# The end of the first expert stage without GpSimd, and the general expert pass in loops

## The chip, the core and the metric

The kernel runs on one core of a Trainium2 chip. A core has five engines that run side by side, each with its own queue: TensorE (PE in the profile; its weight loads are PEld), VectorE (DVE), ScalarE (ACT), GpSimd (POOL) and SyncE (SP, which here only issues DMAs). They meet through semaphores. TensorE multiplies into PSUM, which GpSimd can't read; SBUF holds everything else. The metric is the device time of one execution in microseconds.

## The reference, cut to what matters

A two-layer network works on 256 latent tokens and 256 context tokens of width 1024. Each layer has a mixer (a convolution, an mLSTM and an RG-LRU side by side) and then a mixture of 16 experts, of which each token uses two. The last layer computes the latent tokens alone. What the change touches is the expert part and the sum around it:

```python
def hier_moe(h, w_rg, b_rg, w_re, b_re, w_gate, w_up, w_down):
    ...
    combine = jnp.sum(jax.nn.one_hot(expert_id, N_EXPERTS) * top_w[..., None], axis=1)
    y = jnp.zeros(hf.shape, jnp.float32)
    for e in range(N_EXPERTS):
        ye = (jax.nn.silu(hf @ w_gate[e]) * (hf @ w_up[e])) @ w_down[e]
        y = y + combine[:, e:e + 1] * ye
...
    h_lat = h_lat + mod_lat[5] * hier_moe(v_lat, *moe_p)
    if not last:
        ...
        h_ctx = h_ctx + mod_ctx[5] * hier_moe(v_ctx, *moe_p)
return rms_norm(h_lat, final_g)
```

Everything is float32. `mod[5]` is a gate, one row of 1024 for the latent tokens and one for the context tokens; `h` on the left is the residual.

## The kernel before

The program is written out in the order mixer 0, experts 0, mixer 1, experts 1. Only TensorE's order is the order of the code (`manual_schedule` for PE); the orders of the other engines are made by a planner at build time, from its own costs, with here and there a constraint by hand: `behind(ins)` puts the instructions of a block behind given instructions on the same engine. A `tc.If` over all engines is a border that the planner moves nothing across.

**Tiles.** Tokens lie in tiles of 128: `NT` is 4 in the first expert stage (two of latent tokens, `m = 0`, and two of context tokens, `m = 1`) and 2 in the second. `hs[m]` holds the residual. `bank()` hands out PSUM banks, six in turn in the first stage and four in the second.

**An expert.** The loop over `x` takes the 16 experts one by one. Each has up to 128 slots: its tokens are gathered by a matmul with a one-hot matrix (`gather`, L1253), multiplied with the gate and up weights (`gu`, L1367), evacuated (`evac`), turned (`act`: transposes L1390, Silu, product L1402) and multiplied with the down weights (`down`, L1416). Groups of slots beyond the first 32 or 64 stand in a `tc.If` on the expert's count, on TensorE alone (L1624, L1631, L1637, L1640, L1663, L1670). `store` copies the result and writes it to DRAM (`Yd`) by DMAs of GpSimd's queue (L1484). Weights come through buffers of several kinds, loaded by SP (`ahead`, L1133, L1139) as earlier contents are released.

**The general pass.** Should an expert have more than 128 tokens, `overflow` computes the rest in full, under `tc.If(n_any > P)` (L1490), over all engines. With these inputs no expert has, so the body is jumped over, in both stages. It stands behind expert `OVER = 3`, after its down matmuls, its stores and the loads of later weights, and `gate_rows` (L265, L266), which makes the gate's rows `gr`, stands just ahead of it.

**The stage's end.** The last expert (`wide`) isn't stored. At its start `fetch` (L1566) begins to gather each token's two rows from `Yd` into `yas[i]`; in the first stage two splits of the next mixer's first weights are prepared too: a split makes a rounded high part (ScalarE's copy, L192) and the rest (a subtraction, L192), its first half of rows on VectorE and its second on GpSimd (`whalf`). `take` weighs and adds the two rows (ScalarE L1582, VectorE L1585), multiplies by the gate's row (VectorE L1587) and adds the residual on GpSimd (L1588). The last expert's own result stays in PSUM (`Z`, by `down_w`, L1452); `spread_y` multiplies it by the gate's row into `yt` (VectorE, L1460), and `to_tokens` turns slots into tokens with a one-hot matmul (L1474) and adds this to what `take` left (VectorE, L1476). In the first stage this is done for `m = 0`, then for `m = 1`; the sums of squares (ScalarE, L1702), the normalization (L277, L278, L279, L284) and the transposes of the next layer (L292) follow, with pieces of the modulation (`pump`: matmuls L234 on weights from `w_mod`, loaded by SP's L188) between them. At the end of the kernel the same steps stand written out (L1730, L1731), and the final norm follows.

Where a helper writes an instruction, the profile shows the helper's line.

Of the kernel before, what the change touches and what calls it, by code (L numbers as in the profile page):

```python
# [40 lines left out]
def hybrid_kernel(ctx, tc, x, c, cx, c_ctx, w_mod, b_mod, norm1_g, norm2_g, w_in, conv_w, conv_b, conv_ln_g,  # L41
# [15 lines left out]
    Yd = dram.tile([NE - NPE, P, D], F32, name="Yd", tag="Yd")  # L57
    cnt = [0]
# [1038 lines left out]
    def moe(l, hs, fill):  # L1097
# [4 lines left out]
        with tc.tile_pool(name=f"mo{l}", bufs=1, reuse_waits="tile") as mo, \  # L1102
# [361 lines left out]
            def totals():  # L1464

                return [yas[i][:, 0] if yas and i < taken[0] else hs[i // 2][:, i % 2] for i in range(NT)]
# [20 lines left out]
            def overflow():  # L1487

                n_any = nc.values_load(cnti[0:1, NE:NE + 1], min_val=0, max_val=NTOK)
                with tc.If(n_any > P):  # L1490
                    cw = mt("cw", [P, NT, NE + 1])
                    cw2 = mt("cw2", [P, NT, NE])
                    fh = tmp.tile([P, 2, 512], F32, yp, f"fh{l}")
                    V.memset(cw, 0.0)
                    V.scalar_tensor_tensor(cw[:, :, 0:NE], pm1, float(P) + 0.5, Wt, op0=OP.is_gt, op1=OP.mult)
                    with tc.For_i(0, NE, 1) as ei:
                        def lw(w, k, c0, res=None):
                            wn[0] += 1
                            t = tmp.tile([P, 512], F32, "Y", f"w{wn[0]}")
                            if res is None:  # L1500
                                src = w[l][bass.ds(ei, 1), k * P:k * P + P, c0:c0 + 512].rearrange("o p f -> p (o f)")
                            else:
                                src = w[l][bass.ds(ei, 1)].rearrange("o (h p k) f -> h k p (o f)", h=2, k=4)[k // 4, k % 4]
                            nc.gpsimd.dma_start(t, src)
                            return t

                        for m in range(NT // 2):
                            for w in (w_gate, w_up):
                                pw = [bank(), bank()]
                                for k in range(KC):  # L1510
                                    wk = lw(w, k, 0, 4)
                                    vn = tmp.tile([P, 2, P], F32, "sg", f"vn{m}{k}", 2)
                                    sl = slice(k * P, k * P + P)
                                    ts = slice(2 * m, 2 * m + 2)
                                    V.tensor_tensor(vn, vh[:, ts, sl].bitcast(F32), vl[:, ts, sl].bitcast(F32),
                                                    op=OP.add)
                                    ps = bank([P, 2, P])
                                    for i in range(2):
                                        T.transpose(ps[:, i, :], vn[:, i, :], ident)
                                    vk = tmp.tile([P, 2, P], F32, "hT", f"vk{m}{k}", 3)  # L1520
                                    V.tensor_copy(vk, ps)
                                    for i in range(2):
                                        T.matmul(pw[i], vk[:, i, :], wk, start=(k == 0), stop=(k == KC - 1))
                                for i in range(2):
                                    if w is w_gate:
                                        S.activation(fh[:, i], pw[i], AF.Silu)
                                    else:
                                        V.tensor_tensor(fh[:, i], fh[:, i], pw[i], op=OP.mult)
                            hts = []
                            for i in range(2):  # L1530
                                V.tensor_scalar(fh[:, i], fh[:, i], cw[:, 2 * m + i, 0:1], None, op0=OP.mult)
                                pt = bank()
                                for f in range(4):
                                    T.transpose(pt[:, f * P:f * P + P], fh[:, i, f * P:f * P + P], ident)
                                ht = tmp.tile([P, 512], F32, "t2", f"ft{m}{i}")
                                V.tensor_copy(ht, pt)
                                hts.append(ht)
                            for hf in range(2):
                                py = [bank(), bank()]
                                for k in range(4):  # L1540
                                    wk = lw(w_down, k, 512 * hf)
                                    for i in range(2):
                                        T.matmul(py[i], hts[i][:, k * P:k * P + P], wk, start=(k == 0), stop=(k == 3))
                                sl = slice(512 * hf, 512 * hf + 512)
                                for i in range(2):
                                    hh = hs[m][:, i, sl]
                                    yt = tmp.tile([P, 512], F32, "t2", f"fy{m}{hf}{i}")
                                    V.tensor_tensor(yt, py[i], gr[m][:, sl], op=OP.mult)
                                    V.tensor_tensor(hh, hh, yt, op=OP.add)
                        V.tensor_copy(cw2, cw[:, :, 1:NE + 1])  # L1550
                        V.tensor_copy(cw[:, :, 0:NE], cw2)
# [26 lines left out]
            def take(ts, ws2):  # L1578
                taken[0] += len(ts)
                for i in ts:  # L1580
                    h, y = hs[i // 2][:, i % 2, :], yas[i]
# [14 lines left out]
            for x in range(NE):  # L1596
# [79 lines left out]
                if x == OVER:  # L1676
                    gr = gate_rows(l, 5, mo, "gr", range(NT // 2), NT // 2)
                    overflow()

            if not last:  # L1680
# [4 lines left out]
                g23 = gate((2, 3))  # L1685
                for m in range(2):
# [33 lines left out]
            if last:  # L1720

                ys, tot = spread_y(NE - 1, (0,)), totals()
                xn = tmp.tile([P, 2, D], F32, "t8", "xn")
                ss = [tmp.tile([P, 4], F32, "sm", f"fs{i}") for i in range(2)]
                for i in range(2):
                    for h in range(2):
                        sl = slice(512 * h, 512 * h + 512)
                        hv, o = tot[i][:, sl], xn[:, i, sl]
# [6 lines left out]
                for i in range(2):  # L1735
# [4 lines left out]
                    V.scalar_tensor_tensor(xn[:, i, 512:], tot[i][:, 512:], r, fin[:, 0, 512:], op0=OP.mult, op1=OP.mult)  # L1740
# [70 lines left out]
```

## Time and profile before

| | |
|---|---|
| median of 3 runs | 1186.6 us (1185.05 to 1187.02) |
| the profiled execution | 1188.6 us, of which 1187.0 from the first to the last instruction |
| busy: TensorE, VectorE, ScalarE, GpSimd | 1043.6, 543.1, 363.7, 228.6 us |
| mean DMA rate | 264 GB/s |
| mean granted TensorE clock | 0.961 of full speed |

Times inside the profile count from the first instruction's start. Mixer 0 runs to about 340 us, the first expert stage to about 693, mixer 1 to about 900 and the second expert stage to the end. In timelines, what stands in brackets is the idle time of the engine ahead of the row and what ended it; `PEq` is TensorE's sequencer, and a `PEldq` row is one of its control instructions. The granted clock is given as a share of full speed: 1.00 is 2.4 GHz, 0.50 is 1.2 GHz.

### The profile page before, as it was taken

To read this page: it belongs to the slowest core of one execution; us is meant where nothing else is said; L and a number is where in the kernel's file an instruction comes from. 1 tells how busy PE (TensorE), PEld (TensorE's weight loads), DVE (VectorE), ACT (ScalarE), POOL (GpSimd) and SP (SyncE) were. 2 spreads that over 40 slices of the span, in tenths; PEclk is the share of its full clock that TensorE was granted. 3 is DMA by queue.
4 is the path that set the end of the run, shared out by engine and by line. 5 is a ranking of instruction groups with operands and counts; after the bars stand their busy time and mean duration, and the time that the engine had idled before them with its cause. 6 is when DMAs were issued, how large, how long until landed. Compare 5 with 4: busy or idle time off the path is not lost. (4 is left out here: it accounts for less than half of the span.)

```text
span 1187.0 us, 21561 instructions
## 1 busy us (share of the span) xinstructions
PE 1043.6 (88%) x8655; PEld 721.6 (61%) x8655; DVE 543.1 (46%) x1239; ACT 363.7 (31%) x713; POOL 228.6 (19%) x241
## 2 busy tenths in 40 slices
PE   6999979899999979999999678999887788888876
PEld 4667778799765535445453356789876555455532
DVE  3779987762451111120101789974866211111115
ACT  3545254443331111111111334654542221111202
POOL 3402123414100000000000634112440000000112
PEclk9989999999999989999999889999998998999988
DMA  9734743376878877898987733444679899999980
GB/s 316 226 106 169 255 148 96 107 252 245 261 313 336 320 268 307 306 374 330 345 322 285 247 91 108 141 143 143 214 265 385 328 411 411 413 403 412 413 302 36
DMA packets 144009, 313.19 MB, mean 264 GB/s; under 512 B 26116, under 2 KB 108336, under 8 KB 124032
## 3 DMA queue, kind: packets, MB, share of 16 engines
q1 hardware_dynamic: 128896, 295.74, 67.8%
q0 software_dynamic: 14704, 14.92, 3.9%
q8 instruction: 102, 1.67, 0.6%
q10 hardware_dynamic: 272, 0.57, 0.1%
q14 instruction: 35, 0.29, 0.1%
HBM read 298.25 MB, written 20.71 MB: 269 GB/s over the span
## 5 line engine op out<-in xcount | busy, mean ns | idle before, releaser
L1402 DVE TENSOR_TENSOR hT<-sg,ps 128x256 f32<-128x256 f32 x63 | 24.8, 421 | 321.6 <-ACT sg L1393 321.5
L1367 PE MATMUL X<-w,XT 128*32 128x256 f32 (+1 forms) x2016 | 139.8, 404 | 21.9 <-PEq L1663 7.0
L1484 POOL DMA_DIRECT2D Yd<-Y x90 | 33.3, 385 | 519.6 <-ACT Y L1480 463.7
L1367 PEld LDWEIGHTS X<-w,XT 128*32 128x32 f32 (+1 forms) x2016 | 76.4, 114 | 84.0 <-issue 40.6
L1367 PE MATMUL ps<-w,XT 128*64 128x512 f32 x512 | 115.4, 602 | 11.5 <-PEq L1490 5.9
L1253 PE MATMUL ps<-P,vh 128*128 128x256 f32 x336 | 87.8, 298 | 9.5 <-PEq L1624 8.1
L1367 PEld LDWEIGHTS ps<-w,XT 128*64 128x64 f32 x512 | 43.2, 139 | 79.8 <-issue 62.4
L1253 PE MATMUL ps<-P,vl 128*128 128x256 f32 x336 | 83.0, 283 | 0.0
L1253 PEld LDWEIGHTS ps<-P,vh 128*128 128x128 f32 x336 | 64.3, 191 | 24.4 <-issue 11.8
L1384 ACT COPY gs<-X 128x512 f32<-128x512 f32 x45 | 26.3, 586 | 171.3 <-PEq L1624 57.4
L765 DVE SCALAR_TENSOR_TENSOR acc<-cb,cwh,acc 128x512 f32<-128x512 f32 (+1 forms) x120 | 78.1, 690 | 1.0
L1480 DVE COPY Y<-Y 128x512 f32<-128x512 f32 x30 | 20.8, 692 | 95.8 <-PEq L1663 31.0
L1253 PEld LDWEIGHTS ps<-P,vl 128*128 128x128 f32 x336 | 64.5, 192 | 0.0
L1416 PE MATMUL Y<-w,hT 128*32 128x256 f32 (+1 forms) x912 | 59.2, 391 | 3.8 <-issue 2.2
L234 PE MATMUL ps<-w,cS 128*32 128x256 f32 x768 | 48.8, 393 | 9.9 <-DMA w<-in_w_mod_dram 9.6
L1416 PE MATMUL ps<-w,hT 128*64 128x512 f32 x240 | 54.8, 598 | 0.3 <-DVE hT L1402 0.2
L1390 PE MATMUL ps<-blob,gs 128*128 128x128 f32 x256 | 42.1, 291 | 11.2 <-PEq L1637 3.9
L1416 PEld LDWEIGHTS Y<-w,hT 128*32 128x32 f32 (+1 forms) x912 | 28.9, 112 | 31.1 <-issue 12.6
L1384 ACT COPY gs<-ps 128x512 f32<-128x512 f32 x15 | 8.8, 588 | 123.2 <-PE ps L1367 123.2
L1390 PEld LDWEIGHTS ps<-blob,gs 128*128 128x128 f32 x256 | 28.2, 145 | 27.0 <-issue 16.0
L234 PEld LDWEIGHTS ps<-w,cS 128*32 128x32 f32 x768 | 22.6, 111 | 29.9 <-DMA w<-in_w_mod_dram 10.4
L1393 ACT ACTIVATE sg<-ps 128x256 f32<-128x256 f32 x64 | 24.1, 391 | 38.3 <-PE ps L1390 37.6
(893 smaller groups left out, 2093.5 us busy)
## 6 DMA issues: line engine op xcount, KB each, us to landing
w<-in_w_down_dram SPq DMA_DIRECT2D x58, 1024.0 KB, 12.9
w<-in_w_gate_dram SPq DMA_DIRECT2D x49, 1024.0 KB, 11.5
w<-in_w_mod_dram SPq DMA_DIRECT2D x48, 1024.0 KB, 6.4
w<-in_w_up_dram SPq DMA_DIRECT2D x48, 1024.0 KB, 12.3
w<-in_w_in_dram SPq DMA_DIRECT2D x23, 1024.0 KB, 6.7
w<-in_w_up_dram SPq DMA_DIRECT2D x32, 512.0 KB, 9.1
w<-in_w_gate_dram SPq DMA_DIRECT2D x30, 512.0 KB, 10.0
w<-in_w_out_dram SPq DMA_DIRECT2D x8, 1024.0 KB, 5.5
```

What stands on the lines that cost most here:

```text
L234: T.matmul(ps[32 * j:32 * j + 32, hf * 256:hf * 256 + 256], cS[:, k, :], w[:, k, :], start=(k < 4), stop=(k >= 4))
L765: V.scalar_tensor_tensor(acc[:, ch], src, wcol, acc[:, ch], op0=OP.mult, op1=OP.add)
L1253: T.matmul(ps[:, cc, :], v[:, i, k * P:k * P + P], P2[:, i, :], start=(n == 0), stop=(n == 2 * NT - 1))
L1367: T.matmul(ps[w * t:w * t + w, o0:o0 + q], XT[:, k, c0:c0 + w], ws[2 * g + k // 4][k % 4][:, f0:f0 + q], start=(k == 0), stop=(k == KC - 1))
L1384: S.copy(o, src)
L1390: T.transpose(pt[:, f, :], gs[:, f * P:f * P + P], ident)
L1393: after = [S.activation(sg, pt[:, :, 0:64], AF.Silu).ins]
L1402: after.append(V.tensor_tensor(hT, sg, pt[:, :, 64:128], op=OP.mult).ins)
L1416: T.matmul(ps[w * t:w * t + w, o0:o0 + q], hk, ws[4 + k // 2][k % 2][:, q * t:q * t + q], start=(k == 0), stop=(k == 3))
L1480: (V.tensor_copy if b else S.copy)(Y, ps)
L1484: nc.gpsimd.dma_start(Yd[x, s0:s0 + w, :].rearrange("s (h f) -> h s f", f=q), Y[:, q * c:q * c + q], **({"cond": n_s > s0} if s0 else {}))
```

## The change

1. The split helper takes its engines: the two splits of the first stage's end are computed by VectorE alone, and the list that the last expert's `act` is put behind names the second half in place of the first.
2. `take` no longer adds the residual. `to_tokens` first adds it to the PSUM sum, by a matmul of the identity with `hs`, then multiplies `yt` into the same sum; VectorE's add (L1476) brings in what `take` left. `yt` is made for both `m` in one go, after the first residual matmuls. The end of the kernel does the same.
3. `overflow` and `gate_rows` stand between the last `gather` of expert 3 and its down matmuls, thus ahead of its stores and of the loads behind it.
4. The general pass is written as three nested loops at run time (expert, token tile, slice of the width), over copies of its input and output in DRAM.

```diff
-    def whalf(raw, hi, lo, hf):
+    def whalf(raw, hi, lo, hf, engs=None):
         sl = slice(4 * hf, 4 * hf + 4)
-        return split((V, G)[hf], hi[:, sl], lo[:, sl], raw[:, sl])
+        return split((engs or (V, G))[hf], hi[:, sl], lo[:, sl], raw[:, sl])
...
-        done = [whalf(*r, hf) for hf in range(2)]
+        done = [whalf(*r, hf, order is not None and (V, V)) for hf in range(2)]
         if order is not None:
-            order += [done[1][0].ins, done[0][1].ins]
+            order += [done[1][0].ins, done[1][1].ins]
...
-            def to_tokens(x, ys, src, dst=None):
-                dst = dst or src
-                ts = [2 * m + ii for m in range(NT // 2) if (m, 0) in ys for ii in range(2)]
-                for i in ts:
+            def to_tokens(x, ys, m, dst):
+                pss = {}
+                for i in range(2 * m, 2 * m + 2):
                     for h in range(2):
-                        ps = bank()
-                        T.matmul(ps, pt_[x][:, h, i * P:i * P + P].bitcast(F32), ys[i // 2, h], start=True, stop=True)
+                        pss[i, h] = bank()
+                        T.matmul(pss[i, h], ident, hs[m][:, i % 2, 512 * h:512 * h + 512], start=True, stop=False)
+                ys = ys()
+                for i in range(2 * m, 2 * m + 2):
+                    for h in range(2):
                         sl = slice(512 * h, 512 * h + 512)
-                        V.tensor_tensor(dst[i][:, sl], src[i][:, sl], ps, op=OP.add)
+                        T.matmul(pss[i, h], pt_[x][:, h, i * P:i * P + P].bitcast(F32), ys[m, h], start=False, stop=True)
+                        if dst:
+                            V.tensor_tensor(dst[i % 2][:, sl], yas[i][:, 0, sl], pss[i, h], op=OP.add)
+                return pss
...
                     with tc.For_i(0, NE, 1) as ei:
...
-                        for m in range(NT // 2):
-                            for w in (w_gate, w_up):
-                                pw = [bank(), bank()]
-                                for k in range(KC):
...
+                        with tc.For_i(0, NTOK, P) as ti:
+                            V.memset(fh, 0.0)
+                            with tc.For_i(0, D, P) as ko:
...
                         V.tensor_tensor(y[:, 0, sl], y[:, 0, sl], gr[i // 2][:, sl], op=OP.mult)
-                        box["tk"] = [G.tensor_tensor(y[:, 0, sl], h[:, sl], y[:, 0, sl], op=OP.add).ins]
...
                     gather(pr, 2 * (x % 2) + 1)
+                if x == OVER:
+                    gr = gate_rows(l, 5, mo, "gr", range(NT // 2), NT // 2)
+                    overflow()
                 if x + 1 < NE:
                     n_next = count(x + 1)
...
                 ahead(x + 1)
-                if x == OVER:
-                    gr = gate_rows(l, 5, mo, "gr", range(NT // 2), NT // 2)
-                    overflow()
...
-                    to_tokens(NE - 1, spread_y(NE - 1, (m,)), totals(), hds[m] * 2)
+                    to_tokens(NE - 1, lambda: yts or yts.update(spread_y(NE - 1, (0, 1))) or yts, m, hds[m])
                     if m == 0:
-                        with behind(box["yt"] + box["tk"]):
+                        with behind(box["yt"]):
                             for hf in range(2):
-                                whalf(*box["w0"][1], hf)
+                                whalf(*box["w0"][1], hf, (V, V))
...
-                ys, tot = spread_y(NE - 1, (0,)), totals()
+                pss = to_tokens(NE - 1, lambda: spread_y(NE - 1, (0,)), 0, None)
...
-                        ps = bank()
-                        T.matmul(ps, pt_[NE - 1][:, h, i * P:i * P + P].bitcast(F32), ys[0, h], start=True, stop=True)
-                        V.tensor_tensor(hv, hv, ps, op=OP.add)
+                        V.tensor_tensor(hv, hv, pss[i, h], op=OP.add)
```

## Rows read from the trace of the kernel before

**Rows 1.** Busy time by stretch: busy us (instructions) by engine, granted clock, DMA share, GB/s

```profile
600.00:620.00 20.00, 19.43 (x153) 10.31 (x153) 2.16 (x4) 2.89 (x6) 0.84 (x3) 1.00 0.84 320
...
670.00:680.00 10.00, 6.20 (x8) 2.38 (x8) 8.41 (x13) 4.36 (x8) 6.14 (x3) 0.66 0.61 190
680.00:690.00 10.00, 2.08 (x3) 1.07 (x4) 9.55 (x13) 0.72 (x2) 6.45 (x5) 0.58 0.26 90
...
720.00:740.00 20.00, 16.04 (x76) 12.68 (x75) 19.50 (x40) 8.66 (x11) 6.62 (x4) 0.90 0.17 54
...
960.00:980.00 20.00, 14.52 (x218) 10.11 (x208) 2.99 (x9) 3.96 (x8) 2.75 (x6) 0.96 1.02 408
```

**Rows 2.** Timeline of VectorE, end of the first expert stage: start, length, line, instruction

```profile
659.03 1.22 DVE L192 TENSOR_TENSOR w208l<-w,w208h 128x1024 fp32r<-128x1024 f32 x1
...
664.76 6.38 DVE L1585 SCALAR_TENSOR_TENSOR ya<-ya,ws 128x512 f32<-128x512 f32 x2
...
673.54 2.29 DVE L192 TENSOR_TENSOR w210l<-w,w210h 128x1024 fp32r<-128x1024 f32 x1
...
679.99 1.41 DVE L1585 SCALAR_TENSOR_TENSOR ya<-ya,ws 128x512 f32<-128x512 f32 x2
...
682.52 3.45 DVE L1585 SCALAR_TENSOR_TENSOR ya<-ya,ws 128x512 f32<-128x512 f32 x2
...
690.42 1.42 DVE L284 TENSOR_SCALAR ya<-hn,hr 128x1024 f32<-128x1024 f32 x2 [0.83 <-POOL hr L279]
```

**Rows 3.** Timeline of GpSimd, the same stretch

```profile
665.12 2.37 POOL L192 TENSOR_TENSOR w208l<-w,w208h 128x1024 fp32r<-128x1024 f32 x1
667.45 2.48 POOL L1588 TENSOR_TENSOR ya<-hl,ya 128x512 f32<-128x512 f32 x2
...
682.15 3.27 POOL L1588 TENSOR_TENSOR ya<-hc,ya 128x512 f32<-128x512 f32 x2 [4.11 <-DVE ya L1587]
```

**Rows 4.** Timeline of TensorE, the same stretch

```profile
673.08 6.20 PE L1474 MATMUL ps<-yt,PT 128*128 128x512 f32 x8 [5.04 <-DVE yt L1460]
...
687.92 5.59 PE L1474 MATMUL ps<-yt,PT 128*128 128x512 f32 x8 [8.64 <-DVE yt L1460]
...
693.44 1.93 PE L234 MATMUL ps<-w,cS 128*32 128x256 f32 x32
695.31 1.97 PE L292 MATMUL ps<-blob,ya 128*128 128x128 f32 x16
...
699.93 1.07 PE L234 MATMUL ps<-w,cS 128*32 128x256 f32 x16 [1.65 <-DMA w<-in_w_mod_dram]
```

**Rows 5.** VectorE's groups by line, 658 to 697 us: count, busy, mean ns, idle before

```profile
L1476 DVE TENSOR_TENSOR hn<-ya,ps 128x512 f32<-128x512 f32 x4 | 2.7, 684 | 1.6 <-PE ps L1474 1.6
...
L1379 DVE TENSOR_SCALAR gs<-X,Wc 128x512 f32<-128x512 f32 x1 | 0.8, 751 | 5.3 <-PE X L1367 5.3
```

**Rows 6.** Timeline of all engines, end of the kernel

```profile
1163.18 7.09 PE L1452 MATMUL Y<-w,hT 128*64 128x512 f32 x32
...
1167.83 3.44 DVE L1585 SCALAR_TENSOR_TENSOR ya<-ya,ws 128x512 f32<-128x512 f32 x2
...
1173.13 5.36 PE L1730 MATMUL ps<-yt,PT 128*128 128x512 f32 x8 [2.86 <-DVE yt L1460]
```

**Rows 7.** Timeline of TensorE after the general pass, first stage

```profile
428.80 8.84 PE L1367 MATMUL ps<-w,XT 128*64 128x512 f32 x32 [5.93 <-PEq L1490]
...
447.32 7.09 PE L1367 MATMUL ps<-w,XT 128*64 128x512 f32 x32 [0.31 <-PEq L1670]
```

**Rows 8.** Branches by source line: count, ns min/median/max, first and last start

```profile
L1490 PEldq COMPARE_BRANCH  x2: 6181/6496/6811, 421.6 to 974.8; - x2
...
L1490 POOLq EVENT_SEMAPHORE  x8: 17/43/8762, 437.2 to 986.5; - x8
...
L1631 PEldq COMPARE_BRANCH  x22: 70/177/1847, 345.8 to 631.9; - x22
...
L1624 PEldq COMPARE_BRANCH  x22: 70/184/3558, 922.4 to 1153.1; - x22
```

More of the change, by code (lines that the diff above doesn't have):

```diff
@@ L1490, in overflow @@
                 with tc.If(n_any > P):
-                    cw = mt("cw", [P, NT, NE + 1])
-                    cw2 = mt("cw2", [P, NT, NE])
+                    NX = NE * NT
+                    cw = mt("cw", [P, NX + 1])
+                    cw2 = mt("cw2", [P, NX])
                     fh = tmp.tile([P, 2, 512], F32, yp, f"fh{l}")
                     V.memset(cw, 0.0)
-                    V.scalar_tensor_tensor(cw[:, :, 0:NE], pm1, float(P) + 0.5, Wt, op0=OP.is_gt, op1=OP.mult)
-                    with tc.For_i(0, NE, 1) as ei:
[L1497 to L1505, printed above, removed]
-                        for m in range(NT // 2):
-                            for w in (w_gate, w_up):
-                                pw = [bank(), bank()]
-                                for k in range(KC):
[L1511 to L1537, printed above, removed]
@@ new lines, in overflow, with ot @@
+                    V.scalar_tensor_tensor(cw[:, 0:NX].rearrange("p (e i) -> p i e", i=NT), pm1, float(P) + 0.5, Wt,
+                                           op0=OP.is_gt, op1=OP.mult)
+                    def ot(tag, shape=(P, 512)):
+                        wn[0] += 1
+                        return tmp.tile(list(shape), F32, tag, f"ov{wn[0]}", {"sg": 2, "hT": 3}.get(tag))
+                    zt = ot("t2")
+                    V.memset(zt, 0.0)
+                    for i in range(NT):
+                        for hf in range(2):
+                            sl = slice(512 * hf, 512 * hf + 512)
+                            t = ot("Y")
+                            vs = [v[:, i, sl].bitcast(F32).rearrange("t (k p) -> t k p", k=4) for v in (vh, vl)]
+                            V.tensor_tensor(t.rearrange("t (p k) -> t k p", k=4), *vs, op=OP.add)
+                            nc.gpsimd.dma_start(Vd[i * P:i * P + P, sl], t)
+                            nc.gpsimd.dma_start(Od[i * P:i * P + P, sl], zt)
@@ new lines, in overflow @@
+                    with tc.For_i(0, NE, 1) as ei:
+                        with tc.For_i(0, NTOK, P) as ti:
+                            V.memset(fh, 0.0)
+                            with tc.For_i(0, D, P) as ko:
+                                vn = ot("sg", (P, P))
+                                nc.gpsimd.dma_start(vn, Vd[bass.ds(ti, P), bass.ds(ko, P)])
+                                ps = bank([P, P])
+                                T.transpose(ps, vn, ident)
+                                vk = ot("hT", (P, P))
+                                V.tensor_copy(vk, ps)
+                                for j, w in enumerate((w_gate, w_up)):
+                                    wk = ot("Y")
+                                    nc.gpsimd.dma_start(wk, w[l][bass.ds(ei, 1), bass.ds(ko, P), :]
+                                                        .rearrange("o p f -> p (o f)"))
+                                    pw = bank()
+                                    T.matmul(pw, vk, wk, start=True, stop=True)
+                                    V.tensor_tensor(fh[:, j], fh[:, j], pw, op=OP.add)
+                            S.activation(fh[:, 0], fh[:, 0], AF.Silu)
+                            V.tensor_tensor(fh[:, 0], fh[:, 0], fh[:, 1], op=OP.mult)
+                            V.tensor_scalar(fh[:, 0], fh[:, 0], cw[:, 0:1], None, op0=OP.mult)
+                            pt = bank()
+                            for f in range(4):
+                                T.transpose(pt[:, f * P:f * P + P], fh[:, 0, f * P:f * P + P], ident)
+                            ht = ot("t2")
+                            V.tensor_copy(ht, pt)
@@ L1538, in overflow @@
                             for hf in range(2):
-                                py = [bank(), bank()]
+                                sl = slice(512 * hf, 512 * hf + 512)
+                                py = bank()
                                 for k in range(4):
-                                    wk = lw(w_down, k, 512 * hf)
-                                    for i in range(2):
-                                        T.matmul(py[i], hts[i][:, k * P:k * P + P], wk, start=(k == 0), stop=(k == 3))
@@ L1544, in overflow @@
[L1544 to L1551, printed above, removed]
+                                    wk = ot("Y")
@@ new lines, in overflow @@
+                                nc.gpsimd.dma_start(Od[bass.ds(ti, P), sl], yt)
+                            V.tensor_copy(cw2, cw[:, 1:NX + 1])
+                            V.tensor_copy(cw[:, 0:NX], cw2)
+                    for i in range(NT):
+                        for hf in range(2):
+                            sl = slice(512 * hf, 512 * hf + 512)
+                            yt, hh = ot("t2"), hs[i // 2][:, i % 2, sl]
+                            nc.gpsimd.dma_start(yt, Od[i * P:i * P + P, sl])
+                            V.tensor_tensor(yt, yt, gr[i // 2][:, sl], op=OP.mult)
+                            V.tensor_tensor(hh, hh, yt, op=OP.add)
```

17 lines of the change are left out of this document (12 added, 5 removed).

## The prediction, made before the result

> **What bounds the kernel now.** I read the busy time by stretch first, to learn which resource ends each stage [rows 1]. In the first expert stage (600 to 620 us stands for 430 to 640) TensorE is busy 19.43 of 20 us, while the DMA engines still have 0.84: TensorE bounds it, so an idle TensorE there is paid one to one. At that stage's end (670 to 690) TensorE is busy 6.2 and then 2.1 of 10 us, at a granted clock of 0.66 and 0.58, and VectorE has 8.4 and 9.6 of 10: VectorE bounds the end, and TensorE's clock falls toward its lower level (1.2 of 2.4 GHz) while it waits. In the second layer's mixer VectorE is full (19.50 of 20). In the second expert stage the DMA share is 1.02 (960 to 980): it is bound by weight traffic.
>
> So time saved up to the mixer of layer 1 should move all that follows, the weight loads of the second stage included: they are issued when TensorE frees their buffers, not at a fixed time. Time that TensorE alone saves inside the second stage should vanish.
>
> Next I read VectorE's order at the end of the first stage [rows 2], and beside it GpSimd's [rows 3]. Two L1585 instructions take 1.41 us at 679.99, where GpSimd does nothing; 6.38 at 664.76, under GpSimd's L192 and L1588 (665.12 to 669.93); 3.45 at 682.52, under another L1588 pair (682.15 on). L192 takes VectorE 1.22 us alone and 2.29 at 673.54, where GpSimd does the other half of the same split. VectorE is not long of itself; it is held by GpSimd.
>
> TensorE's timeline then shows what this delays [rows 4]: 5.04 us of standing before the first `to_tokens` (673.08) and 8.64 before the second (687.92), each for `yt` of VectorE, and only at 693.44 the work of the next layer.
>
> **The change, part by part. 1: the end of the first stage.** Removed: eight L1588 additions, and GpSimd's halves of the two splits. From VectorE's line up to the end of L284 (690.42 + 1.42 = 691.84), which the transposes L292 need, go:
> - 6.38 - 1.41 = 4.97 and 3.45 - 1.41 = 2.04, the two stretched L1585 pairs;
> - 2.29 - 1.22 = 1.07, the stretched split;
> - 1.6, VectorE's wait for L1474 between its first four L1476 [rows 5], since those matmuls no longer start on a slow clock.
>
> That is 9.68. Added: two split halves at 1.22, 2.44; the first of them stands ahead of `act` of the last expert by the new ordering list, so TensorE's last `down_w` also starts 1.22 later. The number of `yt`, L1587 and L1476 instructions is the same. L284 then ends at 691.84 - 9.68 + 2.44 = 684.6; should the planner put the four L1476 of the second half ahead of it (0.68 each), at 687.3.
>
> TensorE's own line: it gets eight `ident` matmuls of 128x512 in fp32, which like L1474 are two instructions each. At the full clock one of these takes, by my estimate, 0.44: L1452 does 32 half-width ones, two side by side, in 7.09 [rows 6]. So 16 new and 16 old instructions make 14.1 us. TensorE is free at 673.08 - 5.04 = 668.04, plus 1.22 for the split, and needs nothing but `hs` for the first four: 669.3 + 14.1 = 683.4. All four `yt` are now made together, after L1587 of the first half: the first at 673.08 - 4.97 + 1.22 = 669.3, the last three times 0.68 later (a row's length of L1476), inside the 7.0 us of the first eight `ident` instructions. The clock stays up, as TensorE has no idle stretch left. The pump L234 follows at 683.4 instead of 693.44, its 1.93 ends at 685.3, and L292 starts between 685.3 and 687.3. I take 686, against 695.31: **9.3 us**. The second pump waited 1.65 for its load at 699.93; that load is issued when the first pump frees a buffer, so it moves along. PSUM: in this stage six banks serve four sums, the gate and the last expert's second bank; the second four sums start on what `yt` and the first L1476 free, which costs nothing while L1476 keeps pace (0.68 against 0.88 for a matmul's two instructions). Bounds: 10.5 if the planner puts the early split half into the 5.3 us that VectorE waits ahead of L1379 [rows 5], so that TensorE isn't delayed; 6.5 if it queues all of the second half ahead of L284 and the pump's own work waits for it.
>
> **2: the general pass.** It isn't run, only skipped, in both stages. After the skip in the first stage TensorE stands 5.93 us, and its next 32 matmuls take 8.84 where 7.09 is usual, with 0.31 of standing [rows 7]: the skip costs 5.93 - 0.31 + 8.84 - 7.09 = 7.37. The branch itself takes TensorE's sequencer 6.2 and 6.8 us, by the rows of its line [rows 8]. What it jumps over, by the code, is 544 matmuls and weight loads in the first stage (272 in the second); in loops it is 50, plus loop control that no row shows. Nearest rows: L1631 and L1624 each jump over 128 such instructions, at a median of 0.18 us, and at worst 1.85 in the first stage and 3.56 in the second. I take a usual skip: **7.4 us**; bounds 7.7 (5.93 + 1.75 = 7.68, if nothing at all is left) and 4.1 (7.68 less 3.56).
>
> The Trainium skill ("Runtime: NRT & Kernel Launch", Instruction fetch mechanics) says that an engine holds two pages of 256 instructions and that a taken branch beyond them waits for the target page to be fetched by DMA. By that the old jump always left the window and the new one would hardly ever; the worst cases of 1.85 and 3.56 over 128 instructions differ from it and show that a short jump can wait too. By the rule this term is 7.4, by the worst row 4.1.
>
> What it is moved past: expert 3's down matmuls, its store copies, its three store DMAs on GpSimd, and six weight loads on SP. GpSimd's part of the old skip waited up to 8.76 us, just after the stores had been issued; ahead of them it has only older stores to wait for, so the stores shouldn't come later. SP has nothing in the pass but its branch. The 16 transposes of `gate_rows` are only moved. In the second stage the same skip is covered by the DMA engines (1.02): **0**; without that cover it would give up to 6.2, the branch.
>
> **3: the end of the kernel.** TensorE ends L1452 at 1170.27, waits 2.86 for `yt`, and runs eight L1730 in 5.36 to 1178.49 [rows 6]. The stretched L1585 (3.44) loses 2.03, so `yt` is ready at about 1173.13 - 2.03 = 1171.1, inside the time of the residual's matmuls. Thus come 8 `ident` instructions and 8 L1730 without a gap at 0.44: 1170.27 + 7.0 = 1177.3. **1.2 us** earlier; bounds 2.0 (the whole stretch) and 0.
>
> Sum 9.3 + 7.4 + 0 + 1.2 = 17.9. The profiled execution took 1188.6 (span 1187.0 and 1.6 around it), so 1170.7; the median of the runs is 1186.6, 2.0 lower, so **1168.7**.
>
> **The rivals.**
> - *The skip still waits.* Loop control may be long, or the target may lie badly. For it: 3.56 over 128 instructions. Against: a median of 0.18. The second term is 0 to 4.1, the sum 10.5 to 14.6, the time 1172 to 1176. The worst rows are two of 44 branches, but the loops' control is not to be seen in any: 14 in 100.
> - *The planner orders VectorE badly at the stage's end* (all of the second half ahead of L284, or `yt` late). Only TensorE's order is written out by hand. Half of the first term is lost: 1173.3. 12 in 100.
> - *TensorE becomes the bound of the stage's end.* If `yt` comes late enough for the clock to fall again, 32 instructions at 0.88 take 28.2, the pump starts at 697.5, 4.1 later than now: 1186.6 + 4.1 - 7.4 - 1.2 = 1182. Against: the first 7.0 us need no `yt`. 5 in 100.
> - *Slower.* VectorE's queue in the mixer of layer 1 is laid out anew by the planner, and is 97% busy, so each misplaced group is paid in full. A group that stands for four L1476 costs 2.7; to turn 17.9 into a loss of 2.4, some seven or eight must fall on the path. Against: the work of that stretch and its inputs' order don't change. 1189 or more; 5 in 100.
> - *The gain is taken back by the second stage's loads.* If these ran at their own pace, only the last 1.2 would be left: 1185.4. Against: their release by TensorE. 4 in 100.
>
> **How the numbers follow.** A measurement here tells some 0.2% (2.4 us) from no change. The forecast has 60 in 100; its own range, by the bounds of its terms, is 1166.4 (10.5 + 7.7 + 2.0 = 20.2) to 1176 (6.5 + 4.1 + 0 = 10.6). Below it there is what the second stage's skip gives if its cover has gaps, at most 6.2; less than half of that reaches 1164. Above it the first two rivals, with some of both together, reach 1178; the last three, 14 in 100, stay out. Faster: 60 + 14 + 12 + 5 = 91; same: 4; slower: 5.
>
> **What would show it.** Right: no L1588 and no GpSimd L192 between 650 and 690; L1585 pairs at 1.4 all through; 16 instructions with `hs` on TensorE right after the gate's matmul and no idle time over 2 us until the pump; the pump some 17 us earlier than 693.44 (10 of its own and 7.4 from the skip); a TensorE branch of the general pass under 1 us in the first stage; the second stage's stretch of full DMA as long as now; the last matmul about 1 us nearer to the last L1452. Wrong: a clock near 0.5 in that stretch, L1585 still long with an idle GpSimd, a TensorE branch of several us, or new VectorE waits in the mixer.

## The result, and the profile after

The changed kernel takes 1172.38 us (median of 4 runs, 1171.72 to 1172.74) against 1186.81 for the kernel before on the same chip: ratio 0.9876 [0.9856, 0.9895], 14.4 us less, where 17.9 less (1168.7) was forecast. Its profiled execution has a span of 1170.9 us. It ran twice more beside the experiments: ratios 0.9858 [0.984, 0.9876] and 0.9887 [0.9869, 0.9905].

First the busy time by stretch, which answers to [rows 1]:

```profile
600.00:620.00 20.00, 19.50 (x154) 10.39 (x152) 2.16 (x4) 2.89 (x6) 0.84 (x3) 1.00 0.81 318
...
655.00:660.00 5.00, 4.70 (x14) 1.43 (x16) 3.78 (x8) 4.07 (x4) 2.92 (x3) 0.66 0.90 325
...
720.00:740.00 20.00, 15.91 (x83) 13.55 (x81) 19.34 (x42) 7.68 (x12) 2.83 (x2) 0.74 0.31 95
960.00:980.00 20.00, 16.32 (x228) 11.48 (x221) 2.92 (x5) 4.19 (x8) 2.12 (x6) 0.91 1.02 410
```

```profile
670.00:680.00 10.00, 10.00 (x52) 4.23 (x50) 9.96 (x18) 4.04 (x14) 0.00 (x0) 1.00 0.34 109
680.00:690.00 10.00, 6.65 (x59) 4.83 (x56) 8.31 (x17) 7.98 (x15) 1.42 (x2) 0.83 0.75 238
```

The bounds are those of before, but from 670 to 680 us TensorE and VectorE are both full, at a granted clock of 1.00 where it was 0.66, and GpSimd does nothing. TensorE's timeline at the end of the first stage answers to [rows 4]:

```profile
655.30 1.11 PE L1455 MATMUL Y<-w,hT 128*64 128x512 f32 x1 [1.75 <-DVE hT L1405]
...
664.21 3.68 PE L1473 MATMUL ps<-hl,blob 128*128 128x512 f32 x8
667.72 3.60 PE L1478 MATMUL ps<-yt,PT 128*128 128x512 f32 x8
671.16 3.60 PE L1473 MATMUL ps<-hc,blob 128*128 128x512 f32 x8
674.59 3.60 PE L1478 MATMUL ps<-yt,PT 128*128 128x512 f32 x8
678.12 1.93 PE L237 MATMUL ps<-w,cS 128*32 128x256 f32 x32
681.77 0.33 PE L295 MATMUL ps<-blob,ya 128*128 128x128 f32 x1 [1.72 <-DVE ya L287]
682.43 3.40 PE L295 MATMUL ps<-blob,ya 128*128 128x128 f32 x15 [0.34 <-DVE ya L287]
...
691.46 0.70 PE L519 MATMUL ps<-uh1a,w194h 128*128 128x256 f32 x4 [1.15 <-DVE modc L248]
```

The two waits of 5.04 and 8.64 us are gone; the 32 instructions (L1473 the residual, L1478 the slots) run without a gap. L237, L295 and L519 are before's L234, L292 and L516. VectorE's timeline answers to [rows 2]:

```profile
652.56 2.35 DVE L195 TENSOR_TENSOR w192l<-w,w192h 128x1024 fp32r<-128x1024 f32 x2
...
659.41 1.41 DVE L1599 SCALAR_TENSOR_TENSOR ya<-ya,ws 128x512 f32<-128x512 f32 x2
...
664.39 0.17 DVE L1589 COPY ws<-ps 128x8 f32<-128x8 f32 x1 [2.37 <-PE ps L1587]
...
677.38 2.47 DVE L1480 TENSOR_TENSOR ya<-ya,ps 128x512 f32<-128x512 f32 x4
...
680.96 1.42 DVE L287 TENSOR_SCALAR ya<-hn,hr 128x1024 f32<-128x1024 f32 x2 [0.84 <-POOL hr L282]
```

All four L1599 pairs take 1.41 or 1.42. But both halves of the early split (652.56) stand ahead of the last `hT`, and the planner put the second half's four additions (677.38) ahead of the normalization L287.

TensorE behind the general pass, and the rows of the pass's line, answer to [rows 7, 8]:

```profile
418.02 3.65 PE L1419 MATMUL ps<-w,hT 128*64 128x512 f32 x16 [0.99 <-DVE P L1241]
...
424.15 7.09 PE L1370 MATMUL ps<-w,XT 128*64 128x512 f32 x32 [0.61 <-PEq L1689]
```

```profile
L1495 POOLq EVENT_SEMAPHORE  x8: 17/43/7158, 406.3 to 958.0; - x8
...
L1495 PEldq COMPARE_BRANCH  x2: 208/830/1453, 415.3 to 956.1; - x2
```

The branch of 6.2 and 6.8 us now takes 0.21 in the first stage and 1.45 in the second.

**Where the time came from.** I compare the start of the same TensorE work in the two profiled executions. Just ahead of the pass (408 us) the changed kernel is 0.2 us behind; after it (the next expert's gather) it is 6.6 ahead: the pass gave 6.8. At the start of the last expert it is 6.5 ahead, at the pump L237 15.3, at L295 13.5, at the second pump 11.4, at the mixer's first L519 11.3: the stage's end gave 4.8, after 8.9 at the pump. In the second stage the lead goes from 11.9 to 18.9 at the pass and to 24.6 at 1080 us of before's time, is back to 11.6 at 1117, and is 14.5 at the last expert. What takes it back by 1117 shows in TensorE's waits from 985 to 1110 us of the changed kernel (total, times, longest):

```profile
PE X L1370 <- DMA w<-in_w_up_dram: 8.3, 7, 2.5
```

The kernel before has no such wait there. The end of the kernel:

```profile
1155.67 3.70 PE L1473 MATMUL ps<-hn,blob 128*128 128x512 f32 x8
1159.21 3.60 PE L1478 MATMUL ps<-yt,PT 128*128 128x512 f32 x8
```

From the last L1455 to the last of these are 7.07 us, against 8.22 between L1452's end and L1730's in [rows 6]: 1.15 less.

### The profile page after: what moved, and what is told of

Its sections match the earlier page's. It is cut to its first block, busy times and chain, and to the rows that moved or that the text cites. A ratio compares the mean times of both kernels' runs of the same rounds, so it can differ in the third digit from the quotient of the medians.

```text
span 1170.9 us, 21575 instructions
## 1 busy us (share of the span) xinstructions
PE 1046.3 (89%) x8679; PEld 722.6 (62%) x8679; DVE 533.1 (46%) x1241; ACT 363.0 (31%) x713; POOL 204.1 (17%) x227
## 5 line engine op out<-in xcount | busy, mean ns | idle before, releaser
L1405 DVE TENSOR_TENSOR hT<-sg,ps 128x256 f32<-128x256 f32 x63 | 24.6, 421 | 314.1 <-ACT sg L1396 314.0
L1370 PE MATMUL X<-w,XT 128*32 128x256 f32 (+1 forms) x2016 | 141.3, 397 | 21.8 <-DMA w<-in_w_up_dram 11.9
L768 DVE SCALAR_TENSOR_TENSOR acc<-cb,cwh,acc 128x512 f32<-128x512 f32 (+1 forms) x120 | 81.4, 717 | 1.0
L1419 PE MATMUL Y<-w,hT 128*32 128x256 f32 (+1 forms) x912 | 57.9, 385 | 4.2 <-DVE hT L1405 1.6
L1419 PE MATMUL ps<-w,hT 128*64 128x512 f32 x240 | 54.8, 598 | 1.3 <-DVE P L1241 1.0
L237 PE MATMUL ps<-w,cS 128*32 128x256 f32 x768 | 49.3, 397 | 7.3 <-DMA w<-in_w_mod_dram 7.1
L1419 PEld LDWEIGHTS Y<-w,hT 128*32 128x32 f32 (+1 forms) x912 | 28.3, 110 | 30.9 <-issue 9.9
L237 PEld LDWEIGHTS ps<-w,cS 128*32 128x32 f32 x768 | 22.9, 113 | 27.9 <-DMA w<-in_w_mod_dram 7.6
## 6 DMA issues: line engine op xcount, KB each, us to landing
w<-in_w_down_dram SPq DMA_DIRECT2D x58, 1024.0 KB, 13.5
```

What stands on the lines that cost most here:

```text
L237: T.matmul(ps[32 * j:32 * j + 32, hf * 256:hf * 256 + 256], cS[:, k, :], w[:, k, :], start=(k < 4), stop=(k >= 4))
L768: V.scalar_tensor_tensor(acc[:, ch], src, wcol, acc[:, ch], op0=OP.mult, op1=OP.add)
L1370: T.matmul(ps[w * t:w * t + w, o0:o0 + q], XT[:, k, c0:c0 + w], ws[2 * g + k // 4][k % 4][:, f0:f0 + q], start=(k == 0), stop=(k == KC - 1))
L1405: after.append(V.tensor_tensor(hT, sg, pt[:, :, 64:128], op=OP.mult).ins)
L1419: T.matmul(ps[w * t:w * t + w, o0:o0 + q], hk, ws[4 + k // 2][k % 2][:, q * t:q * t + q], start=(k == 0), stop=(k == 3))
```

## The experiments

Each kernel is the changed one with the edit shown; its ratio is to the kernel before on the same chip. One group takes the general pass apart, the other the stage's end.

**pass_unrolled.** The general pass as it was, unrolled and behind expert 3's stores; the stage's end as changed.

```diff
-                if x == OVER:
-                    gr = gate_rows(l, 5, mo, "gr", range(NT // 2), NT // 2)
-                    overflow()
                 if x + 1 < NE:
...
                 ahead(x + 1)
+                if x == OVER:
+                    gr = gate_rows(l, 5, mo, "gr", range(NT // 2), NT // 2)
+                    overflow()
...
-                    with tc.For_i(0, NE, 1) as ei:
-                        with tc.For_i(0, NTOK, P) as ti:
...
+                    with tc.For_i(0, NE, 1) as ei:
...
+                        for m in range(NT // 2):
+                            for w in (w_gate, w_up):
```

> The changed kernel with the general pass of before: unrolled, and behind expert 3's stores and loads. The stage's end and the kernel's end stay changed. If the skip was worth 7.4 us as the two traces say: 1172.4 + 7.4 = 1179.8 us, with a TensorE branch of 6 to 7 us again in both stages and the second one costing nothing at the end. If the gain came from the stage's end instead (my forecast for it was 9.3 us): 1174 or less.

Measured: 1181.49 us (6 runs), 0.9939 [0.9915, 0.9963]. That is 9.1 us above the changed kernel by the medians, some 7.5 by the two ratios, where 7.4 was expected. The branch is long again, and TensorE's work behind it is 7.45 us later than in the changed kernel:

```profile
L1495 PEldq COMPARE_BRANCH  x1: 6696/6696/6696, 421.9 to 421.9; - x1
```

Against the kernel before, this run keeps only the new ends of the stage and of the kernel. They give 5.6 us by the medians on one chip (4.4 to 10.1 by the ratio's interval), where the forecast had 9.3 + 1.2 = 10.5.

**pass_loops_behind.** The pass in loops, but behind the stores: only the first two hunks of the diff above.

> The changed kernel with the general pass in loops, but at its old place, behind expert 3's stores and loads. If the length of the jump sets the stall: 1172.4 us within 1, the branch under 2 us. If the new place hides the stall (the transposes and the down matmuls behind it being issued late anyway): 1178 to 1180, with a stall of about 6 us on TensorE.

Measured: 1178.32 us (6 runs), 0.9933 [0.991, 0.9955]. TensorE's branch is short, 0.33 us. Yet at expert 4's down matmuls TensorE is 7.1 us behind the changed kernel, and still 6.9 at the last expert's L1455. ScalarE's and TensorE's timelines show where it went:

```profile
430.36 0.59 ACT L1387 COPY gs<-ps 128x512 f32<-128x512 f32 x1 [6.69 <-PE ps L1370]
438.78 0.59 ACT L1387 COPY gs<-X 128x512 f32<-128x512 f32 x1 [7.83 <-DMA Yd<-Y]
```

```profile
439.42 1.12 PE L1393 MATMUL ps<-blob,gs 128*128 128x128 f32 x4 [5.94 <-ACT gs L1387]
```

```profile
L1495 POOLq EVENT_SEMAPHORE  x4: 17/43/43, 437.6 to 437.9; - x4
```

The last fence is GpSimd's part of the skip: it signals only from 437.6 on, when expert 3's stores, issued up to 422, have landed. ScalarE's copy into `gs` waits for that. By the code, the looped pass loads tiles into the slots of `gs` (tag `t2`) and `sg` through GpSimd's queue; the unrolled one only into those of `Y`. So the next writer of a `gs` must wait until GpSimd, though it skips the block, has passed it.

With buffers of its own for these tiles (loops_behind_own_slots) the kernel doesn't fit into SBUF, so there is no time for that form.

**loops_behind_y_slots.** The kernel of pass_loops_behind, with the loop's loads in the slots of `Y`, to try just that.

```diff
-                    zt = ot("t2")
+                    zt = ot("Y")
...
-                                vn = ot("sg", (P, P))
+                                vn = ot("Y")[:, 0:P]
...
-                                yt = ot("t2")
+                                yt = ot("Y")
...
-                            yt, hh = ot("t2"), hs[i // 2][:, i % 2, sl]
+                            yt, hh = ot("Y"), hs[i // 2][:, i % 2, sl]
```

> The general pass in loops, behind expert 3's stores as in pass_loops_behind, but every tile that it loads through GpSimd takes a slot of Y, none a slot of gs or sg. Theory: in pass_loops_behind the jump itself cost 0.2 to 0.3 us on TensorE; the 5.5 us were ScalarE's copy of the gate-and-up result, which stood 7.83 us until GpSimd, itself waiting for expert 3's stores (to 437.6), let go the slot of gs that the skipped block would load. With the loads in Y's slots GpSimd still waits there, but the next writer of a Y comes only at 440: ScalarE's copy waits under 2.5 us, TensorE's work of the next expert stands within 1 us of the changed kernel's, and the time is 1170.5 to 1174. Rival: it isn't the slots (it is the stores themselves, or ScalarE's own branch): ScalarE's copy waits 7 to 8 us again, TensorE loses 4 to 6 us there, and the time is 1176 to 1179.

Measured: 1172.46 us (4 runs), 0.9869 [0.9852, 0.9886]: the changed kernel's time, at the old place. GpSimd waits as long as before, and nobody waits for it:

```profile
432.56 0.59 ACT L1387 COPY gs<-X 128x512 f32<-128x512 f32 x1 [1.93 <-PEq L1653]
```

```profile
L1495 POOLq EVENT_SEMAPHORE  x4: 17/43/43, 437.2 to 437.7; - x4
```

Here the pass gave 7.3 us against the trace of before (at the new place 6.8, where TensorE waits the 0.99 at L1419). The slots are the cause of the loss at the old place; without it the two places take the same time. The unrolled pass at the new place was not tried, nor were the slots of `gs` and of `sg` told apart.

**pass_alone.** The pass as changed, the stage's end with both of the next two edits. It is not quite the end of before: `yt` is still made for both `m` in one go, and the second split is no longer put behind GpSimd's additions (`behind(box["yt"])` without `box["tk"]`).

> The changed kernel with the end of the stage as before: residual by GpSimd, splits by VectorE and GpSimd in halves; only the general pass is the new one, at its new place. Theory: the two edits of the stage's end stand in for one another (residual_on_gpsimd and splits_on_both each have the first matmuls of the next mixer within 1 us of the changed kernel, by their traces): with both undone the mixer's first matmuls come 4 to 5 us later than in the changed kernel, and the time is that of before less the pass's 7.4: 1179 to 1180. Rival: the end of the stage gave little, and the 4.7 us read between the two traces are chance of the clock: the mixer begins within 1.5 us of the changed kernel, and the time is 1172 to 1175.

Measured: 1181.22 us (6 runs), 0.9949 [0.9932, 0.9966]. That is 5.2 us less than before by the medians, 4.0 to 8.1 by the ratio, and above the expected 1179 to 1180. In its trace the pass gives 6.8 again, but the mixer begins at 698.49, 7.0 later than in the changed kernel. VectorE shows why:

```profile
658.29 8.70 DVE L1598 SCALAR_TENSOR_TENSOR ya<-ya,ws 128x512 f32<-128x512 f32 x2
```

```profile
658.67 2.36 POOL L195 TENSOR_TENSOR w192l<-w,w192h 128x1024 fp32r<-128x1024 f32 x1
660.98 2.50 POOL L1601 TENSOR_TENSOR ya<-hl,ya 128x512 f32<-128x512 f32 x2
663.45 2.33 POOL L195 TENSOR_TENSOR w194l<-w,w194h 128x1024 fp32r<-128x1024 f32 x1
```

L1598 (L1599 of the changed kernel) takes 7.29 more than its 1.41, and the three GpSimd groups beside it sum to 7.19. So this end of the stage is itself 2.2 us slower than before's, where GpSimd's second split came only later: TensorE is 6.5 ahead of the kernel before at the last expert, and the mixer begins 4.2 earlier than at 702.73. The 6.8 less these 2.2 make 4.6, near the 5.2 of the medians.

**residual_on_gpsimd.** Residual on GpSimd again, splits on VectorE.

```diff
                         V.tensor_tensor(y[:, 0, sl], y[:, 0, sl], gr[i // 2][:, sl], op=OP.mult)
+                        G.tensor_tensor(y[:, 0, sl], h[:, sl], y[:, 0, sl], op=OP.add)
...
-                        T.matmul(pss[i, h], ident, hs[m][:, i % 2, 512 * h:512 * h + 512], start=True, stop=False)
...
-                        T.matmul(pss[i, h], pt_[x][:, h, i * P:i * P + P].bitcast(F32), ys[m, h], start=False, stop=True)
+                        T.matmul(pss[i, h], pt_[x][:, h, i * P:i * P + P].bitcast(F32), ys[m, h], start=True, stop=True)
```

> The changed kernel with the residual added by GpSimd in the row-weighing step again and no identity matmuls; both splits stay on VectorE. If GpSimd's additions hold VectorE: the weigh-and-add pairs take 3.4 us again where GpSimd adds (1.4 now), TensorE stands idle for yt and its clock falls; 3 to 5 us lost at the first stage's end and 1 to 1.5 at the kernel's end, 1176.5 to 1179 us. If only the splits held it, the 16 instructions fewer on TensorE (6.9 us of its time at the stage's end, 3.5 at the kernel's end) show as a gain: 1170 or less.

Measured: 1176.09 us (5 runs), 0.9911 [0.9888, 0.9933]. Two L1598 pairs take 3.50 and 3.44, and TensorE stands before the transposes:

```profile
683.38 0.48 PE L295 MATMUL ps<-blob,ya 128*128 128x128 f32 x1 [9.87 <-DVE ya L287]
```

Still the mixer begins at 691.78, only 0.3 later than in the changed kernel's profile, and 1.7 later a few matmuls on. TensorE's 16 extra instructions take there the time for which it otherwise waits. But the profiled execution took 1172.8 us, 3.3 below the median of 1176.09, and its clock stayed at 1.00 behind the 1.75 us wait before L1455; what the longer executions lost is in no trace.

**splits_on_both.** Splits shared with GpSimd again, residual on TensorE.

```diff
-        done = [whalf(*r, hf, order is not None and (V, V)) for hf in range(2)]
+        done = [whalf(*r, hf) for hf in range(2)]
...
-                                whalf(*box["w0"][1], hf, (V, V))
+                                whalf(*box["w0"][1], hf)
```

> The changed kernel with both splits halved between VectorE and GpSimd again; the residual stays on TensorE. The second half on VectorE ahead of the last expert's activation cost 1.1 us of idle TensorE and 1.7 us of slow clock; taking it away gives 2.9 us, but the two GpSimd halves then hold VectorE for up to 2.4 us each. By the first alone 1169.5 us, by both 1171 to 1173. If the early half is not what delays TensorE: 1174 or more.

Measured: 1170.6 us (4 runs), 0.9859 [0.9836, 0.9881]: not told apart from the changed kernel. TensorE waits 0.62 instead of 1.75 before L1455, and VectorE pays with one pair of 6.04 beside two GpSimd splits (2.37 and 2.68); the mixer begins at 690.75. By the traces either edit alone brings the mixer's start to within 1 us of the changed kernel, and without both it comes 7.0 later: they are not two gains that add up. The medians agree for the splits, which add nothing that can be told once TensorE adds the residual (1170.6 without them, 1170.6 to 1172.7 with them). Without TensorE's residual the kernel is 3.4 to 5.5 slower by the medians, so how far the splits alone replace it stays open.

**early_split_in_gap.** The early split half is free to run while VectorE waits ahead of `evac`.

```diff
-                gb = evac(x, 1, X2)
                 with behind(box["w0o"] if wide and not last else ()):
+                    gb = evac(x, 1, X2)
                     hA = act(x, 0, ga)
```

> The changed kernel with one constraint more: the evacuation of the last expert's second bank is queued behind the early split, so that both its halves fall into the 5.3 us in which VectorE waits for TensorE. If the second half ahead of the activation cost 2.9 us (1.1 idle, 1.7 slow clock): 1169.5 us, TensorE's idle time ahead of the last expert's down matmuls back at 0.6 and its clock at 1.00 there. If what follows sets the pace (VectorE's normalized rows and splits for the next layer): 1172.4 within 0.7.

Measured: 1169.86 us (5 runs), 0.9862 [0.984, 0.9884]. The half runs at 647.02, in the gap, and TensorE has no wait before L1455, whose matmuls all run at full clock. But only a part of the gain is kept:

```profile
652.87 0.64 PE L1455 MATMUL Y<-w,hT 128*64 128x512 f32 x1
...
679.61 0.48 PE L295 MATMUL ps<-blob,ya 128*128 128x128 f32 x1 [3.63 <-DVE ya L287]
```

4.1 us ahead of the changed kernel at L237, TensorE is 2.2 ahead at L295: it waits for VectorE, 3.63 instead of 1.72. In the mixer it stays 2.1 to 3.5 ahead (up to 757 us; it was 0.6 ahead before the last expert). The median is 0.7 below that of changed_again, run beside it: no measurable gain.

**norm_first and gap_and_norm_first.** The first half's norm is written ahead of the second half's additions, so that the planner needn't put these before L287; then both edits together (this one twice).

```diff
+                        r = rows_of(0)
+                        xs = norm_nat(hds[0], [y[:, 0] for y in yas[0:2]], r)
                 for m, hd in enumerate(hds):
-                    sq = mt(f"hq{m}", [P, 2, 2])
...
+                    if m:
+                        r = rows_of(m)
```

> The changed kernel with the squares, the root and the normalization of the first token half written ahead of the weighing of the second half, so that the planner no longer puts that half's four additions ahead of it. If the late normalization costs 1.7 us of idle TensorE before the transposes and 1.4 us of slow clock in them: 1169.3 to 1170 us, no idle time before the transposes. If the second half's work is then late instead, or VectorE's rows for the next layer set the pace: 1172.4 within 0.7.

> Both of these edits. If the two losses add up: 1172.4 - 2.9 - 2.8 = 1166.7 us, near to my forecast of 1168.7. If one hides the other: 1169 to 1170. If neither is on the path: 1172.

> The kernel of gap_and_norm_first once more, to see whether it beats the changed kernel. If the early split's delay and the late norm cost what their traces show, it stays 1 to 3 us below the changed kernel of the same call (1168 to 1170); if VectorE's work up to the mixer is the bound whatever its order, the two are within 1 us.

Measured, in this order: 1171.33 us, 0.9871 [0.985, 0.9891]; 1168.53, 0.9848 [0.983, 0.9866]; and 1172.16, 0.9879 [0.9862, 0.9896]. L295 starts 2.1, 5.5 and 4.8 us earlier than in the changed kernel, but at the mixer's work of 707 us TensorE is 4.7, 2.4 and 3.6 us behind the changed kernel, and at that of 727 us 2.6 behind, 0.2 ahead and 1.0 behind: the mixer takes it back. VectorE's normalization of the second token half (L287) started at 683.46 in the changed kernel and took 1.42 us; in the three traces it starts at 688.23 to 690.57 and takes 4.25 to 4.28, beside a GpSimd split of 2.4, as here in gap_and_norm_first. By 707 TensorE has waited at L343 for rows of that half, 1.9 to 4.5 us in all; that this late normalization is the whole reason is not shown.

```profile
688.23 4.28 DVE L287 TENSOR_SCALAR xsB<-ya,hr 128x1024 f32<-128x1024 f32 x2 [0.65 <-POOL hr L282]
```

The two runs of the same kernel beside the changed one (1170.59 and 1172.68) differ from it by 2.1 and 0.5 us: no measurable gain.

**changed_again and changed_third.** The changed kernel beside these.

> The changed kernel itself once more, as the point of comparison on this chip: 1172.4 us, 0.988 of the kernel before.

> The changed kernel itself, for the comparison on the same chip: 1170.5 to 1172.5 by its runs so far.

Measured: 1170.59 (5 runs) and 1172.68 (5 runs). In the first one's profile the same 1.75 us wait before L1455 is not followed by a low clock:

```profile
655.00:660.00 5.00, 5.00 (x26) 1.61 (x24) 3.78 (x8) 4.08 (x4) 2.38 (x3) 1.00 1.00 349
```

There the 15 transposes take 1.86 instead of 3.40, and the mixer begins 2.2 us earlier than in the profile shown above. But the low clock comes later instead, under the mixer's first matmuls:

```profile
687.43 1.12 PE L246 MATMUL ps<-blob,mp 128*128 128x128 f32 x4 [2.88 <-ACT mp L240]
689.24 1.19 PE L519 MATMUL ps<-uh1a,w194h 128*128 128x256 f32 x4 [0.69 <-DVE modc L248]
```

```profile
690.00:695.00 5.00, 5.00 (x31) 5.00 (x30) 4.10 (x8) 0.39 (x1) 1.55 (x9) 0.65 0.19 23
```

These take 1.12 and 1.19 where the other profile has 0.66 and 0.70, and from 697 to 707 us the two executions are within 0.1 us of one another. Nothing of the 2.2 is left.

## Why the prediction was right, and which step was not

**The general pass: 7.4 forecast, 6.8 measured, by a reason that was only half of it.** The long jump costs what was said: unrolled it takes 6.7 us and delays TensorE by 7.45; in loops 0.2 to 0.3. With other slots at the old place the pass gives 7.3; at the new place TensorE also waits the 0.99 at L1419. The branch rival fell in the first stage, and in the second its 1.45 is covered. The trace agrees with the rule on taken branches that the prediction cites from the Trainium skill ("Runtime: NRT & Kernel Launch", Instruction fetch mechanics), by the 6.7 against the 0.2 to 0.3. What the long branch waits for no run shows, and the 1.45 of the short one in the second stage stays unexplained. What the prediction left out: it asked whether the new place delays the stores, and took it for neutral otherwise. The loops bring a cost of their own, loads by GpSimd into slots that ScalarE writes next; at the old place this takes back 5.9 us by the medians, and in the trace the whole lead. The new place puts GpSimd's wait (up to 7.16 us here) before the stores, with nobody behind it, or the slots can be chosen, as loops_behind_y_slots shows.

**The stage's end: 9.3 forecast, 4.8 measured. This step failed.** VectorE's sum comes out near: L284 ended at 691.84; less the lead of 6.5, less the 9.68 removed, plus 2.44 for the split halves, plus 2.7 for the four additions ahead of it, is 680.8. L287 ends at 682.38. The missing 1.6 have the size of what the clock cost: after the 1.75 us wait that the early split half makes, L1455 took 8.7 us instead of 7.1 (0.66 from 655 to 660), L1587 came late, and VectorE waited 2.37 for it, against 0.73 in changed_again. The rest fits by luck: of the 1.6 that VectorE waited for TensorE 0.60 stayed, and against that an L278 that took 1.12 us beside GpSimd's additions takes 0.17 now, which the sum had not counted. "The clock stays up, as TensorE has no idle stretch left" was wrong twice: in that wait, and in the 1.72 before the transposes, which then take 3.40. So at L295 7.0 were left: 9.3, less 1.3 for the additions (687.3 instead of 686), less 1.6, plus 0.6 because the transposes start on the first of the two L287. 2.2 more went in the transposes and 0.1 after them, where the pump's load is no longer waited for but ScalarE's and VectorE's pieces of the modulation are. The price of the early half was put at 1.22; it was 1.1 of standing and 1.6 of clock. In changed_again the clock stayed up at L1455 and fell in the mixer instead. A few matmuls into the mixer (712 us of before) the stage's end has given 5.1 in the changed kernel's profile, 4.6 in changed_again and 5.1 in changed_third: not more where the clock stayed up at L1455. Of the case named for the lower bound the additions ahead of L287 came true, but not that the pump waits for them, and its 6.5 did not include the clock.

Behind that lies a wrong picture: the removed stretches were added up as if each were paid. splits_on_both shows no gain from the split edit once the residual is gone from GpSimd. early_split_in_gap shows that a wait for VectorE takes back half of what TensorE gains, and gap_and_norm_first that even an end of the stage that gives all of the forecast (9.9 us at 712 of before, in both traces of that kernel) loses it in the mixer (3.5 and 2.9 are left at 731).

**Second stage: 0, as forecast, up to 1117 us.** TensorE's lead grew by 7 at the pass and was given back to the weight loads. The 2.9 that it gained from there to the last expert are not explained. **Kernel's end:** 1.2 forecast, 1.15 measured; the 0.44 for one identity instruction was 0.43 to 0.44.

**The sum.** 4.8, 6.8 and 1.2 make 12.8; the medians say 14.4. The profiled pair differs by 16.1 in span; the profile of before was 2.0 above its median. The lead that this pair gained between the mixer's start and the last expert, 11.3 to 14.5, I ascribe to nothing: its cause stays open. That the time came out as near to the forecast as it did owes something to these 3.2, which no term names. The slower rivals left no trace; the planner's bad order (12 in 100) came true, next to the likeliest case and not in place of it. Its price, half of the first term, is about what was lost, but the order accounts for only 1.3 of that.

## What to carry to other kernels

A block that is skipped still binds: each tile that it would load through a queue makes the next writer of that slot wait until that queue's engine has passed the block, and this engine may stand for its own earlier stores. When two edits remove the same contention, price each with the other done, and then look at what is next in line. Where an edit leaves TensorE even 1.75 us idle, put the matmuls behind it at both clock levels into the range, and read the gain again some microseconds into the next stage.

## What the runs showed of the hardware

- VectorE is not slowed by GpSimd here but stopped: its pair of 1.41 us grew by 4.63 beside GpSimd splits of 2.37 and 2.68, and by 7.29 beside 7.19 of GpSimd work. The additions that read PSUM were not seen to stretch: in residual_on_gpsimd three L1479 took 1.93 us beside a GpSimd pair of 2.83.
- The Trainium skill ("SBUF — State Buffer", SBUF: two separate sides) says that a VectorE operation with two SBUF inputs and a GpSimd operation that reads SBUF lock each other out for whole instructions. These numbers agree.
- After the same wait of 1.75 us the granted clock fell (0.66 to 0.77 in the 5 us row of the profile behind it) in 6 of 8 profiled executions, the changed kernel's own among them, and stayed at 1.00 in two, changed_again and residual_on_gpsimd. With a wait of 0.62 or none it stayed at 1.00 in all six, the kernel before among them. In changed_again the low clock came some 30 us later, and took back what the first matmuls had gained.
